# Weight sums on VectorE, lag copies on GpSimd, and three more places for weight spills

## The chip, the cores and the metric

The kernel runs on one core of a Trainium2 chip. The metric is the device time of one execution in microseconds (us). TensorE (PE in the profile) multiplies, with its weight loads shown apart (PEld); VectorE (DVE), ScalarE (ACT) and GpSimd (POOL) do the elementwise work; SyncE (SP) only issues DMA transfers, and GpSimd issues transfers as well. Each engine runs its own instructions strictly in the order in which the program gives them, and waits for other engines by semaphores.

## The reference, cut to what matters

One layer of a streaming encoder on a prompt of 2048 rows and 8 samples of 16 rows, with D_MODEL = 1024:

```python
h = rmsnorm(x, ln_g)
proj = h @ w_in                                   # 1024 -> 5120 columns
u_a, z_a, u_b, z_b, g_a, g_b = split(proj)        # 512, 512, 1024, 1024, 1024, 1024
y_a = s5_mixer(u_a)                               # complex diagonal state space, 32 groups
y_a = gelu(y_a); y_a = y_a * sigmoid(y_a @ w_glu + b_glu)
p_a = (y_a * silu(z_a)) @ w_pa
xc = causal_conv(u_b)                             # width 4
y_b = rglru(xc)                                   # block-diagonal gates, then a scan over time
p_b = (y_b * silu(z_b)) @ w_pb
out = x + (sigmoid(g_a) * p_a + sigmoid(g_b) * p_b) @ w_out
```

Outputs are the normed rows and the new states. All products keep about float32 accuracy: every operand is split into a float16 high part and a float16 low part, and each product is three float16 matmuls (high by high, high by low, low by high; lines 161 to 163).

## The kernel before

The work has stages that follow each other on TensorE: the norm and the S5 inputs; the first gate columns (both up to about 219 us of the profile); sixteen pairs (to about 985 us); the product with w_pb, beside which the S5 recurrence runs (to about 1205 us); and the tail with the GLU, w_pa, w_out and the last norm.

**A pair** (`run_pair`) multiplies the normed input by two blocks of 128 columns of w_in. It does so by Strassen-Winograd's scheme with seven products instead of eight (`quad`, once for each half of the prompt), and between the two halves once for the samples. A pair thus has 15 positions: products 1 to 7, the sample at 8, products 9 to 15. Even pairs ("b") make the input and the gate of branch B, odd pairs ("g") make the merge gates and the S5 gate. Two pairs together number their positions 1 to 30, called `place`: 1 to 15 in a b pair, 16 to 30 in a g pair. Each product goes to one of five PSUM banks; after it, ScalarE or VectorE evicts the bank (tiles `ub`, `gs`, `zb`, `sz`), and a later product takes the bank again.

**The weights of the next pair** are made beside it by the generator `w_forms`. It takes the two raw blocks (`wraw`, float32, 512 columns for each quarter A11, A12, A21, A22) and forms the sums that the scheme wants: S1 = A21 + A22, S2 = S1 - A11, S4 = A12 - S2, S3 = A11 - A21. The first three live in the tile `wt`, the last in A21's place in `wraw`. ScalarE makes the high part of each form (`high`, an ACT copy `wf<-wt` or `wf<-wraw`), VectorE the low part (`low`). The four sums are made by `gtt`, on GpSimd (line 56), 64 in the 16 pairs. The generator advances by one step per position, at 8 to 15 and then at the start of the next pair.

**The planner.** At every position `run_pair` calls `tick(2.8 - c)`: c is the cost that the step of `w_forms` gives with its `yield`, plus a fixed cost of evictions; what is left is the budget from which `pump` starts steps of other jobs. Jobs in `tasks` come first: `b_work`, the convolution taps, gates and scan of branch B (one job per b pair and half, and one for the samples). Jobs in `low` take what remains: `w_spill`, which splits 44 blocks of the later weights into high and low and stores them to DRAM (`wr` loaded, `wq` made on ScalarE and VectorE, stored by a GpSimd DMA), and two `s5_prep` generators, which make the matrices of the 16 S5 group pairs. `Later(k)` lets a job rest k positions, `Step(c)` charges c and lets it rest one. The budget decides only in which order instructions are put on the engines' queues.

A job of `s5_prep` makes two outer products on GpSimd (`wb`, `wc`: each four products into the tile and into `t`, and a sum), transposes and small matmuls on TensorE, splits on ScalarE and VectorE, and stores to `sD` and `kpD`. Its `lags` copies the lag kernel `dd`, loaded back from `kpD`, into another order of columns (`d2`, shown as `d<-dd`): two ScalarE copies of 128x512 float16 per group pair, 32 in all, each reading in steps of 16 elements, and then one GpSimd DMA to `sD`.

Two ranges hold jobs back: `w_spill` does not go on while `place` is in `NO_SPILL` (13 to 21), `s5_prep` not while it is in `NO_PREP` (11 to 21). After pair 15 the loop over w_pb starts with `y_load`, which loads branch B's output `Y` from DRAM through SP's queue.

Of the kernel before, what the change touches and what calls it, by code (L numbers as in the profile page):

```python
# [13 lines left out]
MUL, ADD, SUB, MAX, MIN = ALU.mult, ALU.add, ALU.subtract, ALU.max, ALU.min  # L14
# [33 lines left out]
def build(tc, I, O):  # L48
    nc = tc.nc
    V, S, G, PE, SP = nc.vector, nc.scalar, nc.gpsimd, nc.tensor, nc.sync  # L50

    def tt(out, a, b, op):
        V.tensor_tensor(out=out, in0=a, in1=b, op=op)

    def gtt(out, a, b, op):
        G.tensor_tensor(out=out, in0=a, in1=b, op=op)  # L56
# [7 lines left out]
    def stt(out, a, s, b, op0, op1):  # L64
        V.scalar_tensor_tensor(out=out, in0=a, scalar=s, in1=b, op0=op0, op1=op1)  # L65
# [7 lines left out]
    def act(out, a, f, **kw):  # L73
        S.activation(out=out, in_=a, func=f, **kw)  # L74

    def scopy(out, a, scale=1.0):
        act(out, a, AF.Copy, scale=scale)

    with ExitStack() as es:
# [5 lines left out]
        def ps(tag, shape=(P, 512)):  # L85
            tag = "a" if tag == "b" else tag
            bufs = {"mm": 5, "a": 3}[tag]
            return psp.tile(list(shape), F32, tag=tag, name="ps_" + tag, bufs=bufs)
# [113 lines left out]
        def proj(W, n, tag="mm"):  # L202
            p = ps(tag)[:, :TILES[n][1]]
            gemm(p, W, lambda k: hT(n, k), KB)
            return p
# [9 lines left out]
        with ExitStack() as p1x:  # L215
# [328 lines left out]
            for n in range(4):  # L544
# [8 lines left out]
                for m in range(4):  # L553
                    p = proj(lambda k: wua[m][:, k], n)
# [33 lines left out]
                    if n == 3:  # L588
                        SP.dma_start(out=uD[1024 * m:1024 * m + 1024].rearrange("(p t) x -> p (t x)", t=8),
                                     in_=uE[m].rearrange("p t l j c -> p (t l j c)"))  # L590
# [18 lines left out]
        def gt(shape, dt=F32, name="g"):  # L609
            return gp.tile(list(shape), dt, tag="g", name=name, bufs=slots)  # L610
# [156 lines left out]
        def w_half():  # L767
            return page_a("w", (4, 4, 2, P), "wf")
# [4 lines left out]
        def w_forms(raw, W):  # L773

            r1, r2 = raw
            A11, A12, A21, A22 = r1[:, 0:4], r1[:, 4:8], r2[:, 0:4], r2[:, 4:8]
            t = wp.tile([P, 4, P], F32, tag="wt", name="wt", bufs=1)
            for h in range(2):
                W[h] = None

            def high(nm, src):
                h, i = FORMS[nm]
                if W[h] is None:
                    W[h] = w_half()
                scopy(W[h][:, i, :, 0], src, WS)

            def low(nm, src):
                h, i = FORMS[nm]
                stt(W[h][:, i, :, 1], src, WS, W[h][:, i, :, 0], MUL, SUB)

            high("A11", A11)
            gtt(t, A21, A22, ADD)
            yield 0.1
            low("A11", A11)
            high("S1", t)
            yield 0.7
            low("S1", t)
            gtt(t, t, A11, SUB)
            high("A12", A12)
            yield 0.7  # L800
            low("A12", A12)
            high("S2", t)
            yield 0.7
            low("S2", t)
            gtt(t, A12, t, SUB)
            yield 0.7
            high("A21", A21)
            high("S4", t)
            yield 0.2
            low("A21", A21)  # L810
            gtt(A21, A11, A21, SUB)
            low("S4", t)
            yield 1.4
            high("S3", A21)
            high("A22", A22)
            yield 0.2
            low("S3", A21)
            low("A22", A22)
            yield 1.3
# [308 lines left out]
        def busy(no):  # L1128

            return branch_b and place in no  # L1130

        NO_SPILL = range(13, 22)
        NO_PREP = range(11, 22)

        def w_spill():
# [15 lines left out]
            def load(i):  # L1151
                src, _, nk = blocks[i]
                if branch_b:
                    r = gt([P, nk, 512 // nk], name="wr")
                else:
                    r = raw_tile()[:, 0:4].rearrange("p a b -> p (a b)").rearrange("p (k c) -> p k c", k=nk)
                SP.dma_start(out=r, in_=src)
                return r

            nxt = None  # L1160
            for i, (_, dst, nk) in enumerate(blocks):
                done["spill"] = i
                while busy(NO_SPILL):
                    yield Later(1)
# [4 lines left out]
                nxt = None if branch_b or i + 1 == len(blocks) else load(i + 1)  # L1169
                while busy(NO_SPILL):  # L1170
                    yield Later(1)
# [24 lines left out]
        def s5_prep(second):  # L1196

            def lags(q, dd):
                d2 = gt([P, 2, 4, P], F16, name="d2")
                for j in range(2):  # L1200
                    scopy(d2[:, j].rearrange("p a (h t) -> p a h t", t=8),
                          dd.rearrange("p g l (j t h) -> p j (g l) h t", j=2, t=8)[:, j])
                G.dma_start(out=sD[q, :, 2], in_=d2.rearrange("p j a x -> p (j a x)"))
                prepared.add(q)

            dd = None
            while second and not prepared:
                yield Later(1)
            while todo:
# [35 lines left out]
                p = ps("a", (P, 4, P))  # L1245
# [6 lines left out]
                if dd:  # L1252
                    lags(*dd)
# [35 lines left out]
                dd = q, gt([P, 2, 2, 256], F16, name="dd")  # L1289
                for g in range(2):  # L1290
                    for l in range(2):
                        kk = kpD[q, g, :, l, 128:384]
                        SP.dma_start(out=dd[1][:, g, l],
                                     in_=bass.AP(kk.tensor, kk.offset, [list(kk.ap[0]), [-16, 8], list(kk.ap[1])]))
                yield Step(0.4)
            yield Later(4)
            lags(*dd)


# [31 lines left out]
        raw = load_pair(0)  # L1331
        Ws = {0: {}}
        wg = w_forms(raw, Ws[0])
        for n in range(NT):
            if n == 1:
# [17 lines left out]
        def run_pair(i, hook):  # L1353
# [5 lines left out]
            def slot():  # L1359
                nonlocal pos, wg, place  # L1360
                pos += 1
                place = (0 if kind == "b" else 15) + pos
                cost = 0.0
                if pos <= 4:
                    cost += next(wg, 0)
                elif i + 1 < len(order):
                    if pos == 5:
                        Ws[i + 1] = {}
                        wg = w_forms(load_pair(i + 1), Ws[i + 1])
                    elif pos >= 8:  # L1370
                        cost += next(wg)
                hook(pos, cost + EVICT[kind][pos % 8])
# [287 lines left out]
        for n in range(NT):  # L1660
            w = TILES[n][1]
            for m in range(8):
# [4 lines left out]
                p = ps("mm")[:, :w]  # L1667
# [5 lines left out]
                g = gbl.pop(0)  # L1673
# [190 lines left out]
```

## Time and profile before

| what | value |
|---|---|
| median of 3 runs (lowest to highest) | 1551.13 us (1546.92 to 1555.46) |
| the profiled execution: its time, its span | 1549.53 us, 1547.7 us |
| mean granted TensorE clock | 0.979 |
| TensorE matmul busy | 1446.3 us (93%) |
| VectorE busy | 1034.2 us (67%) |
| ScalarE busy | 815.5 us (53%) |
| GpSimd busy | 505.3 us (33%) |

The span runs from the first to the last instruction; the execution's own time has 1.83 us more around it. Busy shares are means over stages with different limits, so the stages are read one by one.

### The profile page before, as it was taken

The page shows a single profiled execution, that of the slowest core. Times are in us where ns is not written, and L with a number is a line of the kernel's source. Part 1 is how long each engine was busy: PE and PEld are TensorE (multiplying, and loading weights), DVE is VectorE, ACT ScalarE, POOL GpSimd, SP SyncE. Part 2 cuts the span into 40 slices and gives each one's busy share as a digit, 9 for nine tenths or more (in the row PEclk, how much of TensorE's full clock was granted, in tenths as well). Part 3 has the DMA queues.
Part 4 walks back from the last instruction along what each step waited for, and adds up shares of the span by engine and source line. Part 5 has one row for each costly group of instructions (what it writes and reads, how often), then busy time and mean ns, then how long its engine had stood idle before and what let it go on. Part 6 is the DMA issues. An engine that isn't in the chain of part 4 may idle for free.

```text
span 1547.7 us, 22800 instructions
## 1 busy us (share of the span) xinstructions
PE 1446.3 (93%) x8168; PEld 724.0 (47%) x8168; DVE 1034.2 (67%) x1913; ACT 815.5 (53%) x1526; POOL 505.3 (33%) x781
## 2 busy tenths in 40 slices
PE   7999999999899999998898899799999899999998
PEld 4544445444444444444443444355555544454444
DVE  5546768867588686887768777444445696665543
ACT  7642446757577575874856758423222562542322
POOL 0790133444536444274363642223332200000000
PEclk9999999999999999999999999899999899999999
DMA  8325223332423424241333241998766772163521
GB/s 207 106 92 208 89 77 93 102 122 86 140 82 109 130 86 140 76 158 61 104 127 92 87 134 69 324 360 292 251 214 221 265 255 72 70 219 107 177 82 55
DMA packets 168490, 222.21 MB, mean 144 GB/s; under 512 B 39258, under 2 KB 117738, under 8 KB 166328
## 3 DMA queue, kind: packets, MB, share of 16 engines
q1 hardware_dynamic: 144440, 150.96, 30.8%
q0 software_dynamic: 23936, 69.79, 12.0%
q8 instruction: 64, 1.05, 0.3%
q14 instruction: 50, 0.41, 0.1%
HBM read 133.85 MB, written 86.84 MB: 143 GB/s over the span
## 4 chain that ended last, share of the span: by engine, by line
PE 48%; issue 15%; DVE 11%; POOL 10%; ACT 7%; DMA 7%; SPq 2%; POOLq 0%; DVEq 0%; ACTq 0%
PE ps_mm L161 11%; PE ps_mm L163 11%; PE ps_mm L162 11%; PE ps_mm L1773 4%; PE ps_mm L1771 4%; PE ps_mm L1772 4%; DVE xc L65 2%; POOL wt L56 2%; POOL t L56 2%; POOL wc L56 1%; POOL wb L56 1%; DVE wf L65 1%; ACT L74 1%; POOL wraw L56 1%; ACT d L74 1%
## 5 line engine op out<-in xcount | busy, mean ns | idle before, releaser
L161 PE MATMUL ps_mm<-T,wf 128*128 128x512 f16 x512 | 198.8, 388 | 34.8 <-ACT gs L74 23.0
L163 PE MATMUL ps_mm<-T,wf 128*128 128x512 f16 x512 | 198.7, 388 | 1.3 <-DVE wf L65 1.3
L162 PE MATMUL ps_mm<-T,wf 128*128 128x512 f16 x512 | 198.6, 388 | 0.0
L162 PEld LDWEIGHTS <-wf 128*128 128x128 f16 x1232 | 121.7, 99 | 151.3 <-issue 46.2
L161 PEld LDWEIGHTS <-wf 128*128 128x128 f16 x1232 | 121.8, 99 | 121.6 <-issue 12.0
L163 PEld LDWEIGHTS <-wf 128*128 128x128 f16 x1232 | 121.7, 99 | 119.9 <-issue 7.0
L161 PE MATMUL ps_mm<-h,wf 128*128 128x512 f16 x448 | 171.2, 382 | 2.0 <-ACT wf L74 2.0
L163 PE MATMUL ps_mm<-h,wf 128*128 128x512 f16 x448 | 170.8, 381 | 0.7 <-DVE wf L65 0.7
L162 PE MATMUL ps_mm<-h,wf 128*128 128x512 f16 x448 | 170.8, 381 | 0.0
L161 PE MATMUL ps_mm<-Y,wpb 128*128 128x512 f16 x256 | 98.0, 383 | 11.0 <-DMA Y<-ybD 11.0
L65 DVE SCALAR_TENSOR_TENSOR gb<-gb,ps_mm 128x512 f32<-128x512 f32 (+1 forms) x40 | 24.3, 607 | 115.3 <-PE ps_mm L163 115.3
L1773 PE MATMUL ps_mm<-wo,M 128*128 128x512 f16 (+2 forms) x264 | 98.0, 373 | 3.4 <-DVE M L65 3.4
L1771 PE MATMUL ps_mm<-wo,M 128*128 128x512 f16 (+2 forms) x264 | 98.0, 373 | 0.0
L1772 PE MATMUL ps_mm<-wo,M 128*128 128x512 f16 (+2 forms) x264 | 98.0, 373 | 0.0
L162 PE MATMUL ps_mm<-Y,wpb 128*128 128x512 f16 x256 | 98.0, 383 | 0.0
L163 PE MATMUL ps_mm<-Y,wpb 128*128 128x512 f16 x256 | 97.8, 382 | 0.0
L74 ACT ACT_TABLE_LOAD x64 | 82.1, 1283 | 3.7 <-PE ps_mm L163 1.8
L65 DVE SCALAR_TENSOR_TENSOR xc<-ub,PC,xc 128x512 f32<-128x512 f32 x96 | 79.9, 832 | 3.2 <-ACT xc L74 1.0
L65 DVE SCALAR_TENSOR_TENSOR wf<-wraw,wf 128x512 f16<-128x512 f32 (+1 forms) x82 | 64.8, 806 | 6.2 <-ACT wf L74 6.1
L65 DVE SCALAR_TENSOR_TENSOR xo<-ps_mm,xo 128x512 f32<-128x512 f32 (+2 forms) x35 | 23.6, 674 | 65.4 <-PE ps_mm L1773 65.4
L1065 POOL DMA_DIRECT2D gbD<-gs x40 | 21.8, 546 | 134.4 <-ACT gs L74 134.3
L74 ACT ACTIVATE yo<-ps_a 128x256 f32<-128x256 f32 x64 | 14.7, 281 | 86.1 <-PE ps_a L1479 86.0
(323 smaller groups left out, 3529.2 us busy)
## 6 DMA issues: line engine op xcount, KB each, us to landing
wraw<-w_in SPq DMA_DIRECT2D x38, 512.0 KB, 4.4
sp<-sD SPq DMA_DIRECT2D x16, 768.0 KB, 4.9
xt<-x_prompt SPq DMA_DIRECT2D x16, 512.0 KB, 4.2
gbD<-gs POOLq DMA_DIRECT2D x32, 256.0 KB, 2.3
ybD<-y POOLq DMA_DIRECT2D x32, 256.0 KB, 2.8
gaD<-gs POOLq DMA_DIRECT2D x32, 256.0 KB, 2.5
Y<-ybD SPq DMA_DIRECT2D x8, 1024.0 KB, 9.9
gb<-gbD SPq DMA_DIRECT2D x32, 256.0 KB, 6.9
```

Of the source, the lines that this page charges most:

```text
L56: G.tensor_tensor(out=out, in0=a, in1=b, op=op)
L65: V.scalar_tensor_tensor(out=out, in0=a, scalar=s, in1=b, op0=op0, op1=op1)
L74: S.activation(out=out, in_=a, func=f, **kw)
L161: PE.matmul(p, lhsT=a[:, 0], rhs=b[:, 0], start=first, stop=False, skip_group_check=more)
L162: PE.matmul(p, lhsT=a[:, 0], rhs=b[:, 1], start=False, stop=False, skip_group_check=more)
L163: PE.matmul(p, lhsT=a[:, 1], rhs=b[:, 0], start=False, stop=last, skip_group_check=more)
L1065: G.dma_start(out=dst[m, :, t0:t0 + w], in_=t)
L1771: PE.matmul(p, lhsT=lh[0], rhs=w_[:, 0, c], start=(k == 0), stop=False)
L1772: PE.matmul(p, lhsT=lh[0], rhs=w_[:, 1, c], start=False, stop=False)
L1773: PE.matmul(p, lhsT=lh[1], rhs=w_[:, 0, c], start=False, stop=(k == KB - 1))
```

## The change

The four sums of `w_forms` go from GpSimd (`gtt`) to VectorE (`tt`), and the cost that each of those steps reports to the planner rises by 0.6. The range in which spills rest shrinks from places 13 to 21 to places 15 to 20, so that they may go on at 13, 14 and 21 too. The two copies in `lags` go from ScalarE to GpSimd.

```diff
             high("A11", A11)
-            gtt(t, A21, A22, ADD)
-            yield 0.1
+            tt(t, A21, A22, ADD)
+            yield 0.7
             low("A11", A11)
             high("S1", t)
             yield 0.7
             low("S1", t)
-            gtt(t, t, A11, SUB)
+            tt(t, t, A11, SUB)
             high("A12", A12)
-            yield 0.7
+            yield 1.3
             low("A12", A12)
             high("S2", t)
             yield 0.7
             low("S2", t)
-            gtt(t, A12, t, SUB)
-            yield 0.7
+            tt(t, A12, t, SUB)
+            yield 1.3
             high("A21", A21)
             high("S4", t)
             yield 0.2
             low("A21", A21)
-            gtt(A21, A11, A21, SUB)
+            tt(A21, A11, A21, SUB)
             low("S4", t)
-            yield 1.4
+            yield 2.0
...
-        NO_SPILL = range(13, 22)
+        NO_SPILL = range(15, 21)
...
                 for j in range(2):
-                    scopy(d2[:, j].rearrange("p a (h t) -> p a h t", t=8),
-                          dd.rearrange("p g l (j t h) -> p j (g l) h t", j=2, t=8)[:, j])
+                    G.tensor_copy(out=d2[:, j].rearrange("p a (h t) -> p a h t", t=8),
+                                  in_=dd.rearrange("p g l (j t h) -> p j (g l) h t", j=2, t=8)[:, j])
```

## Rows read from the trace of the kernel before

**Rows 1.** Windows: us, busy (instructions) of each engine, clock, DMA share, GB/s.
```profile
219.00:985.00 766.00, 711.91 (x3949) 348.16 (x3948) 575.55 (x869) 513.94 (x900) 352.03 (x453) 0.98 0.34 110
985.00:1205.00 220.00, 210.02 (x1388) 115.96 (x1387) 102.39 (x324) 60.25 (x185) 67.94 (x112) 0.98 0.78 271
```
**Rows 2.** TensorE's waits: us in total, times, longest.
```profile
PE ps_mm L161 <- ACT gs L74: 23.0, 11, 5.8
PE ps_mm L161 <- DMA Y<-ybD: 11.0, 2, 9.3
PE ps_mm L161 <- ACT ub L74: 10.3, 7, 3.5
PE ps_a L162 <- DVE xs L53: 7.3, 4, 4.3
```
**Rows 3.** All engines' waits, two of them.
```profile
ACT wf L74 <- POOL wt L56: 48.7, 27, 4.9
...
POOL sD L1203 <- ACT d L74: 27.0, 12, 4.2
```
**Rows 4.** Timeline of ScalarE in pair 13: start, us, [idle before, releaser].
```profile
872.74 0.63 ACT L74 ACTIVATE wf<-wt 128x512 f16<-128x512 f32 x1 [4.68 <-POOL wt L56]
...
878.21 2.13 ACT L74 ACTIVATE d<-dd 128x512 f16<-128x512 f16 x2
880.24 0.59 ACT L74 ACTIVATE gs<-ps_mm 128x512 f32<-128x512 f32 x1
```
**Rows 5.** Timeline of GpSimd in the same stretch.
```profile
866.30 1.75 POOL L56 TENSOR_TENSOR wc<-par 128x256 f32<-128x256 f32 x2
...
871.44 1.26 POOL L56 TENSOR_TENSOR wt<-wraw 128x512 f32<-128x512 f32 x1
```
**Rows 6.** Timeline of TensorE: first and last of nine waits.
```profile
391.70 0.58 PE L161 MATMUL ps_mm<-T,wf 128*128 128x512 f16 x1 [5.83 <-ACT gs L74]
...
929.22 0.38 PE L161 MATMUL ps_mm<-T,wf 128*128 128x512 f16 x1 [3.49 <-ACT ub L74]
```
**Rows 7.** Windows right behind two of those waits, columns as in rows 1.
```profile
880.90:884.40 3.50, 3.50 (x9) 1.29 (x9) 2.25 (x4) 3.47 (x6) 3.48 (x6) 0.50 0.40 151
391.70:396.70 5.00, 5.00 (x12) 1.72 (x12) 2.02 (x4) 4.38 (x8) 4.91 (x7) 0.50 0.26 105
```
**Rows 8.** Groups by line and form: busy us, mean ns | idle before.
```profile
L56 POOL TENSOR_TENSOR wt<-wt,wraw 128x512 f32<-128x512 f32 x16 | 25.7, 1609 | 26.3 <-DVE wf L65 26.2
...
L56 POOL TENSOR_TENSOR wt<-wraw 128x512 f32<-128x512 f32 x16 | 21.1, 1318 | 14.2 <-DMA wraw<-w_in 14.1
```
**Rows 9.** The same view, ScalarE and VectorE.
```profile
L74 ACT ACTIVATE d<-dd 128x512 f16<-128x512 f16 x32 | 34.4, 1127 | 0.8 <-DMA dd<-kpD 0.8
L53 DVE TENSOR_TENSOR gs<-ps_mm,gs 128x512 f32<-128x512 f32 x48 | 32.8, 684 | 16.7 <-PE ps_mm L163 16.4
...
L53 DVE TENSOR_TENSOR ga<-ga,mb 128x512 f32<-128x512 f32 x32 | 22.1, 692 | 1.7 <-DMA mb<-mbD 0.6
```
**Rows 10.** Tiles sz and wq: ns shortest/median/longest, first and last start.
```profile
L65 DVE SCALAR_TENSOR_TENSOR sz<-sz,zb x16: 675/1218/2172, 237.2 to 939.6; 128x512 f32<-128x512 f32 x16
...
L74 ACT ACTIVATE wq<-wr x38: 612/620/637, 222.1 to 986.1; 128x512 f16<-128x512 f32 x38
L65 DVE SCALAR_TENSOR_TENSOR wq<-wr,wq x38: 676/683/3319, 222.9 to 988.7; 128x512 f16<-128x512 f32 x38
```
**Rows 11.** Groups of GpSimd with no second input.
```profile
L386 POOL MEMSET zt<- 128x1024 f16 x1 | 1.0, 953 | 0.0
...
L434 POOL COPY pw<-stk 128x64 f32<-128x64 f32 x1 | 0.3, 299 | 0.0
...
L484 POOL COPY m16c<-SQ 128x16 f32<-128x16 f32 x1 | 0.2, 200 | 0.0
```
**Rows 12.** Timeline of SP's queue at the end of pair 15.
```profile
983.86 2.46 SPq L1293 DMA_DIRECT2D dd<-kpD  x4
986.37 1.14 SPq L1545 DMA_DIRECT2D Y<-ybD  x2
```

## Prediction

> **What bounds the kernel now.** I read the windows by stage first. TensorE is the bound almost everywhere, so what counts is where it stands still. Beside the product with w_pb it is busy 210 of 220 us, in the sixteen pairs 712 of 766 [rows 1]: 54 us of idle time lie in the pairs, and all that the change touches lies there too, save the last six spills. The list of TensorE's waits comes next: most of that idle time is a product that waits for ScalarE to evict its bank (23.0 us for `gs`, 10.3 for `ub`), the rest in part VectorE's `xs` (7.3) [rows 2]. So the question is what makes ScalarE late. In the list of all waits it stands 48.7 us, 27 times, for GpSimd's sum `wt` [rows 3]. The timeline of pair 13 shows how that reaches TensorE. GpSimd runs the second outer product `wc` from 866.30, and the sum that was put on its queue behind it starts at 871.44 [rows 5]. ScalarE waits 4.68 us for it with every eviction queued behind; later the two lag copies take 2.13 us directly ahead of the eviction of `gs` [rows 4], and TensorE stands 5.14 us until 880.88.
>
> I went through TensorE's timeline for the pairs in this way. Nine waits have, in the 9 us ahead of them, a ScalarE wait for a sum or an outer product of GpSimd; the first is 5.83 us and the last 3.49 [rows 6], and the nine sum to 28.2 us. Six of them are followed by a stretch at a granted clock of 0.50, which is 1.2 GHz, the lower of the two levels; the two shown last 3.5 and 5.0 us [rows 7]. A stretch at half clock loses half its length, so six of these lengths lose 10.5 to 15 us; some are shorter, and I take 11.5. Behind these waits stand some 40 us.
>
> **The sums on VectorE.** 64 sums leave GpSimd, in four groups whose means run from 1.32 to 1.61 us [rows 8]: 64 x 1.47, some 94 us. On VectorE the same form, `ga<-ga,mb` with two float32 inputs in SBUF, takes 0.69 us [rows 9]: 64 x 0.69 = 44 us more on an engine that is busy 575 of 766 us in this stage [rows 1].
>
> Part of this comes back. `sz<-sz,zb` with both inputs in SBUF takes 0.675 us at its shortest, 1.218 in the median and 2.172 at the longest, and `wq` 0.683 against 3.319 [rows 10]; `gs<-ps_mm,gs`, one input in PSUM, has a mean of 0.684 [rows 9]. The long ones of the timeline lie over GpSimd's tensor_tensor. So each sum on GpSimd now holds up VectorE's two-input work. VectorE runs 75% of the time; if it stood still for all of that share of 94 us, moving the sums would give back 70 us, if for none of it nothing. I take 40, since the longest rows show a hold for a whole GpSimd instruction but many of VectorE's have an input in PSUM. Net VectorE gains 4 us of work, between 44 more and 26 less.
>
> On the path: the sum follows a `low` on the same queue, so it needs no hop between engines, and the outer products no longer stand in front of it. The nine waits lose their cause. Not all is won: GpSimd's second sum stood 26.2 us of its idle time waiting for VectorE's `low` [rows 8], so VectorE's own lag stays in the chain, and ScalarE's head-of-line wait becomes a wait for VectorE. I leave a quarter of the 28.2 us in place: 7 us. Queued behind each sum are taps, splits and evictions. Where VectorE is late already, at the gates in b pairs (`xs`, four waits, longest 4.3 [rows 2]), one sum in front costs 0.69 in each of 8 b pairs: 5.5 us. If instead two of the four sums lay on the path in all 16 pairs it would be 22 us; if none, nothing.
>
> **The planner's costs.** The nine steps of `w_forms` report 6.0 before and 8.4 after. Two pairs have 30 x 2.8 = 84 of budget; less two `w_forms` and the fixed evictions (10.7) that leaves 61.3, now 56.5. `b_work` needs 37.1 of it by its own costs, spills 44 / 8 x 1.0 and two preps 2 x 3.6, together 12.7. It still fits, so the jobs move by single positions and none falls out; the added VectorE work displaces other work instead of piling up on it. Price 0. If the last prep slips, its loads of `dd` stand in front of `Y` on SP's queue, as they do today by 2.5 us [rows 12], and TensorE already waits 11.0 us for `Y` [rows 2]: each position of slip would add 2.6 us, and a slip past `y_load` would put `Y` first and give back up to 11. I take 0, with both ends kept.
>
> **The lag copies on GpSimd.** ScalarE loses 32 copies of 1.127 us, 34.4 us [rows 9]. What one costs on GpSimd no row shows. From below, the memset writes 1024 elements in 0.953 us, so 0.48 us for 512; the two copies of 64 and 16 elements give 0.099 / 48 = 2.06 ns for an element [rows 11] and so 0.200 + 496 x 0.00206 = 1.22 us; from above, the slowest group of two-input sums, 1.61 us [rows 8]. I take the copies' value: 32 x 1.22 = 39 us, between 15 and 52. GpSimd then has 94 - 39 = 55 us less to do. It used to wait 27.0 us for ScalarE's copies before the DMA to `sD` [rows 3]; that wait goes, and the copies take about its place. What stands behind them are the next `wc` and the stores. The DMA itself is hidden: `sD` is read only after 985 us. The relief of ScalarE is already in the nine waits (pair 13 has both causes), so I count it once, at nothing extra; uncovered, it would be worth up to 2.13 us where the copies stand ahead of an eviction.
>
> The Trainium skill speaks against this part ("SBUF — State Buffer", § Who interferes with whom): a VectorE instruction with two SBUF inputs contends with a GpSimd instruction that reads SBUF, and the second to issue blocks until the first is done. The long `sz` rows agree for tensor_tensor [rows 10]; for a GpSimd copy no run here shows it. By it the copies too would hold VectorE's two-input work; without it they would cost VectorE nothing.
>
> **The spills.** 38 of 44 blocks are split in the pairs, each 0.62 us of ScalarE and 0.68 of VectorE [rows 10], one load on SP's queue and one store on GpSimd's. With 24 of 30 places open instead of 21, the other six should move into the pairs. Beside the w_pb product they cost nothing today, as TensorE is busy there; in the pairs they cost 6 x 0.68 = 4 us if all lay on the path. VectorE's 190 us of idle time cover them: price 0.
>
> **The sum.** 1549.5 - 28.2 - 11.5 + 7 + 5.5 = 1522.3 us for the profiled execution. The median of the runs is 1.6 us above that execution: 1524.
>
> **The rivals.** *Half eaten.* VectorE's lag takes over ScalarE's wait, and reordering makes new waits at other places. For: the `low` in front of each sum, and `xs` late already. Against: in pair 13 and at others of the nine places VectorE stood idle itself, waiting for ScalarE in its turn. Half to all of 40 us is lost: 1531 to 1551, 1541 at the middle.
>
> *More than forecast.* With GpSimd lighter by 55 us the waits for `wb` and `wc` go too, taps shorten, and `Y` slips in front: 54 + 13 us is the ceiling, of which half of what my forecast leaves would give about 1503.
>
> *VectorE becomes the bound (the other side).* Two of four sums in each pair lie on the path, held by the outer products (2.17 us as the longest `sz` instead of 0.69): 16 x 2 x 0.69 to 2.17 = 22 to 69 us; and the lag copies hold VectorE as the sums do now, for up to 75% of their 39 us, 29 us. Against the 40 us won this ends between 1533 and 1610; with 65 us of new waits it is 1576. It turns slower once the new waits exceed 40 us, 2.5 per pair. For it: an engine 75% busy that gets more to do, and taps that GpSimd already stretches. Against it: the 40 us handed back, and the budget that makes room.
>
> **How the numbers follow.** Forecast (1510 to 1536) 0.45; half eaten 0.22; more than forecast 0.12; VectorE bound 0.21. The range reaches from 1500, about where the larger gain lies, over all of the second case to 1557, leaving out some 0.04 below and 0.16 above. A difference under 0.5%, 8 us, is about what this kernel's measurement can't tell from no change. Faster by more than that, below 1543: all of the forecast, all of the larger gain and half of the second case, 0.68. Same: the other half and 0.05 of the third, 0.16. Slower, above 1559: 0.16.
>
> **What would show it.** Right: `ACT wf <- POOL wt` is gone from the waits and what replaces it, `ACT wf <- DVE wt`, is under 25 us; TensorE's wait for `gs` falls below 10 us; fewer stretches at clock 0.50 in the pairs; `sz<-sz,zb` nearer 0.7 us; lag copies near 1.2 us; VectorE's busy time in the pairs within 25 us of 575; all spills before 985. Wrong: TensorE's waits for `xs` or for VectorE's evictions grow beyond 20 us, or VectorE is over 620 us busy; the lag copies take 2 us or more; `Y` starts later behind `dd`.

## The result, and the profile after

The changed kernel takes 1524.52 us (median of 4 runs, 1523.57 to 1527.46); the kernel before takes 1551.02 (4 runs). The ratio is 0.9832 with a 95% interval of 0.9801 to 0.9862. The profiled execution of after took 1527.46 us with a span of 1525.7, against 1547.7.

The 22.0 us between the two spans come from the pairs. Read from TensorE's timeline (first and last products of each stage), the pairs take 733.8 us instead of 765.9, 32.1 less. The stages ahead, in which only the first two of the 64 sums lie, ended 5.5 us later in this execution, at 223.2 us; that varies between executions, as e7_no_lags, the same kernel up to there, ended them at 218.5; the gap between the last pair's product and the first with `Y` grew from 9.7 to 13.3 us; the w_pb stage and the tail differ by -0.1 and +1.2.

The windows of the pairs and of the w_pb stage, which answer to [rows 1]:

```profile
223.00:957.00 734.00, 705.04 (x3943) 346.24 (x3939) 576.65 (x923) 482.34 (x864) 279.73 (x405) 0.98 0.34 111
957.00:1195.00 238.00, 221.40 (x1559) 126.40 (x1559) 113.66 (x341) 65.29 (x196) 91.25 (x143) 0.97 0.81 281
```

VectorE has 54 instructions more in the pairs and is busy 576.65 us, 1.1 more than before. GpSimd gives up 72 us, ScalarE 32.

TensorE's waits (us in total, times, longest), which answer to [rows 2]:

```profile
PE ps_mm L161 <- DMA Y<-ybD: 10.1, 2, 8.9
PE ps_a L162 <- DVE xs L53: 7.7, 3, 3.7
PE ps_mm L161 <- DVE gs L53: 7.3, 3, 4.3
...
PE ps_mm L161 <- ACT gs L74: 5.3, 1, 5.3
...
PE ps_mm L161 <- ACT ub L74: 0.2, 1, 0.2
```

The waits for ScalarE's `gs` and `ub`, 33.3 us before, are 5.5. `xs` stands where it stood; TensorE's wait for VectorE's part of `gs` has grown to 7.3 (1.4 in the pairs before). In the list of all waits ScalarE no longer waits for GpSimd's `wt` (48.7 us in [rows 3]), but for VectorE's:

```profile
ACT wf L74 <- DVE wt L53: 17.1, 16, 3.8
```

Tiles of after (ns shortest/median/longest, first and last start), for [rows 10] and the operation that no row of before had:

```profile
L65 DVE SCALAR_TENSOR_TENSOR sz<-sz,zb x16: 676/683/1074, 241.3 to 909.7; 128x512 f32<-128x512 f32 x16
...
L1201 POOL COPY d<-dd x32: 1096/1116/1581, 314.0 to 1013.4; 128x512 f16<-128x512 f16 x32
...
L74 ACT ACTIVATE wq<-wr x37: 612/617/634, 229.1 to 965.7; 128x512 f16<-128x512 f32 x37
L74 ACT ACTIVATE wq<-wraw x7: 612/629/632, 997.1 to 1124.4; 128x512 f16<-128x512 f32 x7
```

`sz` is back at its shortest. A lag copy takes 1.12 us in the median. But the spills did not move in: 37 blocks are split from `wr` in the pairs (38 before), and the last of the seven behind them begins at 1124.4.

So the number came out as forecast. Whether it came by the forecast steps, only the parts can tell.

### The profile page after: what moved, and what is told of

The parts are those of the page before. It is cut to its first block, busy times and chain, and to the rows that moved or that the text cites. A ratio compares the mean times of both kernels' runs of the same rounds, so it can differ in the third digit from the quotient of the medians.

```text
span 1525.7 us, 22740 instructions
## 1 busy us (share of the span) xinstructions
PE 1445.7 (95%) x8168; PEld 726.4 (48%) x8168; DVE 1043.5 (68%) x1977; ACT 785.1 (51%) x1494; POOL 446.1 (29%) x749
## 3 DMA queue, kind: packets, MB, share of 16 engines
q1 hardware_dynamic: 144440, 150.96, 31.1%
q0 software_dynamic: 23936, 69.79, 12.3%
## 4 chain that ended last, share of the span: by engine, by line
PE 69%; DVE 11%; DMA 6%; ACT 5%; issue 5%; POOL 3%; SPq 1%; DVEq 0%; POOLq 0%; ACTq 0%
PE ps_mm L161 17%; PE ps_mm L163 17%; PE ps_mm L162 17%; PE ps_mm L1773 4%; PE ps_mm L1772 4%; PE ps_mm L1771 4%; DVE wf L65 1%; ACT L74 1%; DMA xt<-x_prompt 1%; ACT yh L74 1%; DVE xc L65 1%; DMA kpD<-kf 1%; DMA Y<-ybD 1%; DMA wraw<-w_in 1%; SPq L1293 1%
## 5 line engine op out<-in xcount | busy, mean ns | idle before, releaser
L162 PEld LDWEIGHTS <-wf 128*128 128x128 f16 x1232 | 121.4, 99 | 126.1 <-issue 18.9
L161 PE MATMUL ps_mm<-Y,wpb 128*128 128x512 f16 x256 | 97.7, 382 | 10.1 <-DMA Y<-ybD 10.1
L74 ACT ACTIVATE gs<-ps_mm 128x512 f32<-128x512 f32 (+1 forms) x92 | 48.3, 534 | 34.9 <-PE ps_mm L163 31.1
```

Source lines behind the costliest of these rows:

```text
L161: PE.matmul(p, lhsT=a[:, 0], rhs=b[:, 0], start=first, stop=False, skip_group_check=more)
L162: PE.matmul(p, lhsT=a[:, 0], rhs=b[:, 1], start=False, stop=False, skip_group_check=more)
```

## The experiments

The change is cut into four: **S**, the sums on VectorE (`gtt` to `tt`); **C**, the costs in the `yield` lines of `w_forms`; **L**, the lag copies on GpSimd; **P**, the three more places for spills. In the table, "effect" is (ratio - 1) x 1552 us, the median of before in these comparisons. "Pairs" and "w_pb" are lengths of stages from TensorE's timeline. "Idle" sums TensorE's waits of over 0.3 us in the pairs. "Half clock" sums what its successive 128x512 products there lose by starting about 0.43 us apart instead of 0.216. The last four are worked out from the trace of one execution each.

| kernel | parts | median | ratio (95%) | effect | pairs | w_pb | idle | half clock |
|---|---|---|---|---|---|---|---|---|
| before | none | 1552 | 1 | 0 | 765.9 | 224.5 | 53.0 | 14.9 |
| e1_sums | S | 1542.97 | 0.9939 (0.9917, 0.9960) | -9.5 | 755.7 | 226.2 | 41.4 | 14.3 |
| e3_lags | L | 1561.44 | 1.0067 (1.0047, 1.0088) | +10.4 | 774.3 | 224.1 | 56.0 | 19.6 |
| e2_costs | C | 1553.74 | 1.0006 (0.9990, 1.0023) | +0.9 | 750.4 | 236.8 | 46.8 | 5.9 |
| e4_spill | P | 1551.70 | 0.9993 (0.9977, 1.0010) | -1.1 | 765.3 | 224.6 | 51.1 | 16.0 |
| e9_engines_only | S L | 1550.86 | 0.9981 (0.9964, 0.9997) | -2.9 | 763.2 | 227.0 | 45.0 | 19.2 |
| e5_sums_costs | S C | 1551.37 | 0.9985 (0.9975, 0.9995) | -2.3 | 750.8 | 237.1 | 37.3 | 15.2 |
| e8_order_only | C P | 1533.34 | 0.9876 (0.9854, 0.9897) | -19.2 | 741.4 | 224.2 | 36.6 | 9.1 |
| e6_no_spill_part | S C L | 1536.13 | 0.9897 (0.9881, 0.9914) | -16.0 | 737.0 | 238.0 | 29.8 | 12.0 |
| e7_no_lags | S C P | 1520.08 | 0.9788 (0.9765, 0.9811) | -32.9 | 729.5 | 224.6 | 27.9 | 6.7 |
| after | S C L P | 1524.52 | 0.9832 (0.9801, 0.9862) | -26.1 | 733.8 | 224.4 | 28.4 | 10.8 |
| e10_dummy | S + load | 1553.65 | 1.0011 (0.9994, 1.0027) | +1.7 | 765.0 | 225.5 | 48.7 | 17.0 |
| e12_dummy_new_order | S C P + load | 1527.81 | 0.9833 (0.9809, 0.9858) | -25.9 | 739.2 | 223.3 | 31.1 | 11.6 |
| e11_y_early | S C P, `Y` early | 1517.53 | 0.9762 (0.9743, 0.9782) | -36.9 | 729.9 | 230.6 | 28.3 | 7.0 |

**e1_sums: the sums alone.** The four `gtt` become `tt`, the costs stay:

```diff
-            gtt(t, A21, A22, ADD)
+            tt(t, A21, A22, ADD)
             yield 0.1
...
```

> The kernel before with the four weight sums on VectorE and nothing else: the planner's costs stay as they were, so every engine's order is that of before, with 64 sums moved from GpSimd's queue into VectorE's. Theory (ScalarE's wait for sums that stand behind outer products on GpSimd is the cause): ScalarE's wait for wt falls from 48.7 us to under 25, TensorE's for gs from 23.0 to under 10, the time by 15 to 35 us (ratio 0.977 to 0.990). Rival A (the gain comes from the planner putting the work in another order): under 8 us, ratio above 0.995. Rival B (VectorE becomes the bound unless the planner makes room): slower than before, ratio above 1.005.

9.5 us are won, a third of what the prediction gave this part, and a size between the ranges of the recorded theory and of rival A. TensorE's waits and the window of the pairs:

```profile
PE ps_a L162 <- DVE xs L53: 18.2, 5, 5.3
...
PE ps_mm L161 <- ACT ub L74: 9.6, 7, 3.1
...
PE ps_mm L161 <- ACT gs L74: 5.6, 11, 2.2
```
```profile
218.00:974.00 756.00, 712.81 (x3960) 348.89 (x3958) 574.03 (x930) 512.38 (x899) 264.80 (x393) 0.98 0.34 111
```

The wait for `gs` goes as forecast, 23.0 to 5.6. VectorE has 61 instructions more in the pairs and is busy 574.03 us where it was 575.55, so the 40 us that were to come back came back. But `xs` grows from 7.3 to 18.2. The longest of its waits, 5.32 us in pair 12, on the timelines of VectorE and of GpSimd:

```profile
813.62 1.12 DVE L65 SCALAR_TENSOR_TENSOR wf<-wt,wf 128x512 f16<-128x512 f32 x1
814.78 1.01 DVE L53 TENSOR_TENSOR wt<-wt,wraw 128x512 f32<-128x512 f32 x1
815.71 1.75 DVE L53 TENSOR_TENSOR xs<-xc,xs 128x512 f16<-128x512 f32 x1
```
```profile
813.11 2.12 POOL L56 TENSOR_TENSOR t<-par 128x256 f32<-128x256 f32 x2
815.31 1.60 POOL L56 TENSOR_TENSOR wb<-wb,t 128x512 f32<-128x512 f32 x1
```

The sum stands directly ahead of `xs`, and GpSimd's outer product, which is not moved, lies over all three and stretches `xs` to 1.75 us. And the clock falls behind such a wait as it fell behind those for ScalarE: the window right after the 4.29 us for `xs` in pair 10 is at 0.50, the lower level (1.2 GHz).

```profile
711.10:715.50 4.40, 4.40 (x11) 1.49 (x11) 4.29 (x10) 2.73 (x6) 0.58 (x1) 0.50 0.08 27
```

So the half-clock loss stays: 14.3 us, 14.9 before.

The orders of all engines are those of before, so each of the prediction's nine waits can be looked up at its own product. Together they are 28.2 us before and 8.3 here.

**e10_dummy: is it that GpSimd is free of the sums?** As e1_sums, and GpSimd is given its load back without the dependence: four additions of a small tile of zeros beside each sum, which nothing reads.

```diff
+            for _ in range(4):
+                gtt(dmy, dmy, dmy, ADD)
             tt(t, A21, A22, ADD)
```

> As the kernel with the sums alone on VectorE, but beside each sum GpSimd gets four idle additions of 80 float16 zeros on a tile of its own, together about 1.4 us, at the place in its queue where the sum was; nobody waits for them. GpSimd's load and its hold on VectorE's second input stay about as before, ScalarE's wait for GpSimd is gone. Theory (the queue wait is the cause): at most a third of the gain of the sums alone is lost. Rival C (the gain is VectorE set free from GpSimd's sums): at least two thirds of it are lost.

The whole gain goes (+1.7, interval from -0.9 to +4.2), though nothing reads what is added. The load is larger than the one taken away: GpSimd is busy 132 us longer in the pairs than in e1_sums, where the sums had taken 87. VectorE is busy 10.5 us longer. TensorE's waits:

```profile
PE ps_a L162 <- DVE xs L53: 14.3, 5, 4.7
PE ps_a L172 <- POOL wb L56: 11.8, 3, 6.8
```

By the total this is rival C's case, but the waits say otherwise. At the nine products TensorE waits 11.6 us here (28.2 before, 8.3 in e1_sums), so most of what ScalarE's wait for the sums had cost stays won. The loss lies elsewhere. Most of it is `wb`, 11.8 us for 2.2 in e1_sums: outer products that come late on GpSimd's own queue. Before, with the real sums on that queue, TensorE waited only 2.8 us for `wb`, so the additions, half as much load again, are no fair stand-in for the sums. If the loss of 11.2 us is scaled from 132 us to 87, 7.4 of the 9.5 us that the sums gave would be GpSimd's lighter load; that is an estimate that takes the loss as proportional to the load, which no run shows.

**e3_lags: the lag copies alone.**

```diff
-                    scopy(d2[:, j].rearrange("p a (h t) -> p a h t", t=8),
-                          dd.rearrange("p g l (j t h) -> p j (g l) h t", j=2, t=8)[:, j])
+                    G.tensor_copy(out=d2[:, j].rearrange("p a (h t) -> p a h t", t=8),
+                                  in_=dd.rearrange("p g l (j t h) -> p j (g l) h t", j=2, t=8)[:, j])
```

> The kernel before with the lag copies on GpSimd and nothing else; orders unchanged. Theory: ScalarE is 36 us less busy, GpSimd's sums come later by about 2.4 us where copies stand ahead of them, so the nine waits stay: within 6 us of before (ratio 0.996 to 1.004). Rival D (the copies ahead of evictions were the larger cause of late banks): 10 us faster or more. Rival E (the copies hold VectorE): 8 us slower or more.

10.4 us slower. The window of the pairs, then two waits of TensorE and one of ScalarE:

```profile
218.00:993.00 775.00, 718.92 (x3964) 350.03 (x3962) 608.64 (x867) 484.09 (x870) 385.49 (x485) 0.97 0.33 109
```
```profile
PE ps_mm L161 <- ACT gs L74: 20.0, 11, 4.4
...
PE ps_a L161 <- DVE wbT L65: 8.0, 3, 3.9
```
```profile
ACT wf L74 <- POOL wt L56: 66.9, 32, 4.9
```

Rival E is met. VectorE has two instructions fewer than before and is busy 33 us longer. The copies' hold can be seen at single instructions, here of VectorE and of GpSimd:

```profile
936.69 2.89 DVE L53 TENSOR_TENSOR xs<-xc,xs 128x512 f16<-128x512 f32 x1
```
```profile
936.88 2.14 POOL L1201 COPY d<-dd 128x512 f16<-128x512 f16 x2
```

`xs`, both inputs in SBUF, takes 0.68 us in the median with GpSimd idle, and 2.89 over two copies. Fifteen such instructions lie over copies and no other GpSimd operation; together they last 18.9 us longer than the medians of their kind. `gs<-ps_mm,gs`, one input in PSUM, keeps its 0.69 us over a copy. ScalarE's wait for sums grows from 48.7 to 66.9, since the copies stand ahead of them, and TensorE waits 8.0 us for VectorE's `wbT` (1.9 before).

**e9_engines_only: S and L, orders unchanged.** The diffs of e1_sums and e3_lags together.

> Sums on VectorE and lag copies on GpSimd, with the planner's costs and the spill places of before: orders unchanged, so this is the change without its reordering. Theory: as the sums alone or up to 8 us faster, since ScalarE's copies stood ahead of evictions in four of the nine waits; ratio 0.975 to 0.988. Rival A (reordering makes the gain): ratio above 0.993.

-2.9 us: the copies take 6.5 of the 9.5 that the sums give. What the two moves between engines do by themselves is a tenth of the result, as rival A has it; the rest comes only with the planner's edits.

**e2_costs, e4_spill, e8_order_only: the planner's half.** All instructions stay on their engines. e2_costs has the first hunk below, e4_spill the second, e8_order_only both.

```diff
-            yield 0.1
+            yield 0.7
...
-            yield 1.4
+            yield 2.0
...
-        NO_SPILL = range(13, 22)
+        NO_SPILL = range(15, 21)
```

> The kernel before with only the planner's costs of the changed kernel. Costs and spill places together gave 19 us with no move between engines, while with sums and costs but the old places the last spill came at 1207 us and the w_pb stage took 237 us instead of 224. Theory 3 (the costs spread the two preps and the branch work more evenly, which helps the pairs, but push spills out of them, which the new places bring back): the pairs are 10 us or more shorter than 766, the w_pb stage 8 to 14 us longer, the total within 10 us of before. Rival H (the places alone make the gain): the pairs take over 760 us.

> The kernel before with only the new range of spill places. Theory 3: spills fit in the pairs already, so the places bring little by themselves: within 8 us of before, ratio 0.995 to 1.005. Rival H (the places alone make the gain): 12 us faster or more, ratio under 0.992.

> The planner's costs and the spill places of the changed kernel, but sums on GpSimd and lag copies on ScalarE as before: the reordering without the moves between engines. Theory 2: ScalarE still waits for sums, TensorE's waits for gs stay above 15 us, within 8 us of before (ratio 0.995 to 1.005). Rival A (reordering makes the gain): 15 us faster or more, ratio under 0.990.

Each alone gives nothing; together they give 19.2 us. The costs shorten the pairs by 15.5 us (6.2 of idle time and 9.0 of half clock) and lose 12.3 of it in the w_pb stage, as theory 3 has it. The tile `wq` and TensorE's waits of e2_costs show where:

```profile
L74 ACT ACTIVATE wq<-wr x33: 612/614/642, 227.1 to 972.9; 128x512 f16<-128x512 f32 x33
L74 ACT ACTIVATE wq<-wraw x11: 612/630/631, 996.2 to 1208.7; 128x512 f16<-128x512 f32 x11
```
```profile
PE ps_mm L161 <- ACT yh L74: 14.4, 1, 14.4
PE ps_a L172 <- POOL wb L56: 14.1, 6, 2.7
PE ps_mm L161 <- ACT gs L74: 10.7, 6, 3.8
```

The dearer steps leave less budget for `low`, and 11 blocks instead of 6 are left behind the pairs. There they go one at a time, (1208.7 - 996.2) / 10 = 21 us apart. The generator of the tail goes on only when all are done (`while len(tasks) > 1 or done["spill"] < 44`, line 1627), so `yh` is 14.4 us late. With the three places open, 37 blocks fit into the pairs, the last of the others begins at 1131.2, and the w_pb stage is back at 224.2.

The pairs' own gain is one of order: one block fewer is split there than before, and the pairs are 24.5 us shorter. ScalarE waits for GpSimd's sums as long as before, and still TensorE's waits for `gs` are a third, against theory 2, which had them above 15 us (all waits of e8_order_only, then TensorE's timeline at the longest and ScalarE's just ahead of it):

```profile
ACT wf L74 <- POOL wt L56: 50.8, 27, 6.3
...
PE ps_mm L161 <- ACT gs L74: 7.9, 2, 5.4
PE ps_mm L161 <- ACT ub L74: 7.1, 5, 3.8
```
```profile
485.84 0.59 PE L161 MATMUL ps_mm<-T,wf 128*128 128x512 f16 x1 [5.45 <-ACT gs L74]
```
```profile
482.68 0.58 ACT L74 ACTIVATE wbT<-ps_a 128x512 f16<-128x512 f32 x1
483.16 2.15 ACT L74 ACTIVATE d<-dd 128x512 f16<-128x512 f16 x2
485.21 0.58 ACT L74 ACTIVATE gs<-ps_mm 128x512 f32<-128x512 f32 x1
```

I placed the starts of the outer products among the positions. Before, pairs 3, 11 and 13 have one at place 24 or 25 and another at 28; those are the pairs with the waits of 5.83, 4.13 and 5.14 us ahead of the product at place 28. With the new order pair 5 alone has that pattern, and the 5.45 us above are pair 5 ahead of place 28; the next there is 2.41 us. The second outer product starts only when the wait is over (in pair 13 at 881.75, TensorE's product at 880.88), so it is the mark of a second prep, not what the bank waits for. What that prep puts on ScalarE is what stands there: in all four pairs its split `wbT` and two lag copies run directly ahead of the late eviction, and the wait for a sum comes some 7 us earlier. The two causes can be taken apart at the three products, as e1_sums and e3_lags keep the orders: without the wait for GpSimd's sums 0.90, 0.00 and 2.20 us are left, without the copies on ScalarE 3.82, 2.10 and 3.43. That the new order wins by keeping the second prep out of such g pairs is argued from the match; no kernel moves a prep alone.

**e5_sums_costs, e6_no_spill_part, e7_no_lags: pairs of parts and one left out.** e5 is S and C, e6 is after without P, e7 is after without L, each with the hunks shown above.

> The kernel before with the sums on VectorE and the planner's costs of the changed kernel; lag copies and spill places as before. The sums alone gave 9 us: TensorE's waits for gs fell from 23.0 to 5.6 us, but its waits for xs grew from 7.3 to 18.2. Theory 2 (the move pays when the planner also makes room on VectorE for it): the xs waits fall back under 10 us and the gain is 18 to 30 us, ratio 0.981 to 0.988. Rival F (the spill places carry the rest): about the sums alone, ratio 0.991 to 0.997.

> The changed kernel with the old range of spill places. Theory 2: the places are worth little, within 6 us of the changed kernel, ratio 0.979 to 0.989. Rival F (the places carry much of the gain): 10 us or more slower than the changed kernel, ratio above 0.990.

> The changed kernel with the lag copies back on ScalarE. They cost 9 us when moved alone and 8 us when moved beside the sums. Theory 2, with the copies' price the same here: 5 to 10 us faster than the changed kernel, ratio 0.976 to 0.981. Rival G (with ScalarE's queue free of GpSimd's sums, the relief of ScalarE shows): slower than the changed kernel by 4 us or more, ratio above 0.986.

e5_sums_costs fails both of its ranges: 2.3 us are won, and `xs` is still 15.8. Without P the w_pb stage is 237 to 238 us in both e5 and e6 (14.6 and 14.8 us of waiting for `yh`): P is worth 10.1 us in the whole change (e6 to after), near rival F's size: 13.6 in the w_pb stage and 3.2 in the pairs, some of it given back in the gap before `Y` and in the start. With L left out P is worth three times as much, 30.6 us (e5 to e7), and 21.3 of them are in the pairs: 9.4 of idle time and 8.5 of half clock. In e5 and e6 each of the six b pairs from pair 4 on has a wait for `xs` of 2.3 to 3.9 us at place 12; with P two such waits of over 2 us are left in e7 and in after. Why the spill places do this is not traced. Without L the kernel is 4.4 us faster by the medians, 6.8 by the ratios, whose intervals touch at 0.9801 and 0.9811; theory 2 had 5 to 10. Its pairs are 4.3 us shorter, and VectorE is busy 558.72 us there for 576.65. At one product after waits 5.34 us where e7 waits 2.45, here on the timelines of GpSimd, ScalarE, VectorE and TensorE:

```profile
543.93 2.95 POOL L1201 COPY d<-dd 128x512 f16<-128x512 f16 x2 [4.03 <-PE ps_mm L163]
...
548.25 2.13 POOL L1201 COPY d<-dd 128x512 f16<-128x512 f16 x2
...
546.92 0.81 ACT L74 ACTIVATE xc<-ub,PC 128x512 f32<-128x512 f32 x1 [3.05 <-POOL d L1201]
...
547.76 4.75 DVE L65 SCALAR_TENSOR_TENSOR xc<-ub,PC,xc 128x512 f32<-128x512 f32 x3 [1.84 <-ACT xc L74]
...
552.12 0.59 PE L161 MATMUL ps_mm<-T,wf 128*128 128x512 f16 x1 [5.34 <-ACT gs L74]
```

By the profile ScalarE's first tap waits for a pair of copies, with the eviction of `gs` queued behind it, and TensorE stands 5.34 us. The three taps on VectorE take 4.75 us over the second pair of copies.

**e12_dummy_new_order: e10's load in the new order.** e7_no_lags with the added lines of e10_dummy.

> Sums on VectorE, costs and spill places of the changed kernel, lag copies on ScalarE, and the idle additions on GpSimd beside each sum again. Without the additions this took 1520.1 us, with the sums on GpSimd 1533.3. Theory 4 (GpSimd's load itself is what the sums cost, by its hold on VectorE and by the lateness of its other work; ScalarE's wait is the smaller part): at least half of the 13 us is lost, 1526 us or more. Theory 1 again (ScalarE's wait for the sum): under a third is lost, 1524 or less.

In the new order S is worth 13.7 us (e8 to e7), and the idle additions take 7.0 of them back (0.9788 to 0.9833; the intervals touch at 0.981). They load GpSimd with 123 us, where the sums had taken 98 (347.16 us busy in e8, 249.11 in e7), and VectorE's busy time grows by 1.3 us only. Theory 4 is met, by little. In proportion to the load, an estimate as above, GpSimd's lighter load would be 5.6 of the 13.7. Where it acts is not shown: TensorE's waits for `wb` and `xs` are those of e7 (6.4 and 9.5 us, 6.2 and 9.6 there), and what grows is idle time in many places, 3.2 us, and half clock, 4.9. What makes up the other 8 us of S in this order is not taken apart either.

**e11_y_early: the first load of `Y` ahead of the last `dd`.** e7_no_lags with

```diff
-            if pos == 13:
+            if pos == 11:
                 y_load(0)
```

> Sums on VectorE, costs and spill places of the changed kernel, lag copies on ScalarE, and the first load of Y two positions earlier (11 instead of 13), ahead of the last prep's loads of dd on SP's queue. Theory (Y waits there behind dd, which waits for a store): TensorE's wait for Y falls from 8.5 us to under 3, the time by 5 to 11 us to 1509 to 1515, ratio 0.972 to 0.976. Rival (the 6 MB of loads bound it): Y lands no earlier, ratio as without it, 0.979.

SP's queue of e11_y_early has `Y` first now:

```profile
942.44 1.24 SPq L1545 DMA_DIRECT2D Y<-ybD  x2
...
952.66 2.56 SPq L1293 DMA_DIRECT2D dd<-kpD  x4
```

The gap to the first product with `Y` falls from 14.5 to 7.7 us, but the w_pb stage grows by 6.0, and 2.6 us are won by the medians, with intervals that overlap: the forecast of 1509 to 1515 is missed, though TensorE's wait for `Y` falls under 3 us as it said. What was hidden behind the wait shows behind it, an outer product first:

```profile
972.43 0.42 PE L1274 MATMUL ps_a<-wc,par 128*32 128x128 f32 x1 [3.35 <-POOL wc L56]
```

By its median it is the fastest kernel of the study, and ahead of after with intervals that don't meet (up to 0.9782, from 0.9801).

## Why the prediction was right, and where it was not

The forecast of 1524 us is met, within the narrow range too, but not by its steps: that it hits the median is luck. Its two prices were -27.2 for the sums and 0 for the rest. Along one path through the runs (none, C P, S C P, all) the parts are -19.2 for the planner, -13.7 for the sums and +6.8 for the lag copies, -26.1 in all. Three errors cancel. The split depends on the path: by none, S, S C, S C P, all it is -9.5, +7.2, -30.6 and +6.8. No part has a price of its own that holds beside every other.

**The nine waits: right.** With the sums alone they fall from 28.2 to 8.3 us, and 7 were to be left (all waits for `gs` and `ub` fall from 33.3 to 15.2). The cause that was named is borne out: in e10_dummy, with GpSimd's queue loaded otherwise, the nine are 11.6. But the gain is not S's alone. At the same nine products e8_order_only, with the sums still on GpSimd, waits 2.6 us, and e2_costs 4.9: the new order takes these waits away as well, and they can be won only once.

**The `xs` waits: half.** +5.5 was forecast for 0.69 us of a sum in each b pair; +10.9 came (e1_sums), since the outer products hold VectorE as well, and the sum and `xs` are stretched. In after `xs` is 7.7 us; the order that C and P make together keeps it down, as the kernels with S that lack one or both have 18.2, 17.0, 15.8 and 20.7 (e1, e9, e5, e6).

**The half clock: wrong in size.** -11.5 was counted as won with the nine waits; -0.6 came with the sums alone and -4.1 in after. The low clock followed the waits for `xs` as it had those for `gs` (0.50 behind both), so the waits that replaced the old ones brought it along. The sum of idle time does not tell how much: e2_costs has 46.8 us of it and 5.9 of half clock, after 28.4 and 10.8. This is the most mis-sized of the four terms that had a price.

**VectorE's balance: right.** 44 us added and 40 given back were to make +4; e1_sums measures -1.5, with 61 instructions more.

**The planner's costs and the spills at price 0: the step that failed.** "It still fits, so the jobs move by single positions and none falls out", and from that "Price 0". Blocks do fall out (33 instead of 38 in the pairs, e2_costs), which costs 12.3 us behind the pairs, and the new order is worth 15.5 us in them; with P, e8_order_only wins 19.2 us where the sum had nothing. The sum of the budget, 56.5 us for 49.8 of work, said that all fits; it could not say which step meets which. That "the other six should move into the pairs" failed too: seven stay out. P keeps C from pushing out more, and it changes the order in the pairs (9.0 us shorter beside C, e2 to e8).

**The lag copies at price 0: wrong.** Their duration was right (1.12 us in the median against 1.22). They cost 10.4 us alone, 6.5 beside S and 4.4 to 6.8 in the whole. VectorE is busy 33 us longer in e3_lags, 23 in e9_engines_only (beside e1_sums) and 18 in after (beside e7_no_lags); the bound was 29. That is what spoke against them: by the Trainium skill's "SBUF — State Buffer", § Who interferes with whom, a VectorE instruction with two SBUF inputs contends with a GpSimd instruction that reads SBUF. The traces agree for a copy (2.89 us for 0.68 in e3_lags). The hold was left to the rival in which VectorE becomes the bound; it belonged into the sum.

**The rivals.** The total is that of the forecast case. "Half eaten" is what the sums alone do (1543), and "more than forecast" is not reached. VectorE as the bound is what e9_engines_only comes near: S and L by themselves end at 0.9981, 2.9 us and so inside the 8 us that the prediction would not tell from no change. **`Y`** stayed behind `dd`, with its gap 3.6 us longer; e11_y_early shows that of the up to 11 us named for it 2.6 were there to be had.

**The signs.** Of those named as right, all came but one: ScalarE's wait for `wt` of GpSimd is gone, the wait for `wt` of VectorE is 17.1 (under 25), `gs` for ScalarE 5.3 (under 10), `sz` 0.683, the copies 1.12, VectorE 1.1 us from 575.55, and half clock is less, if by less than counted; but the spills are not all done before 985. None of those named as wrong came, except that `Y` is a little later. The signs could not tell where the gain was from: e8_order_only has `gs` under 10 as well, with every instruction on its old engine.

**Open.** L beside S and C without P helps by 13.7 us (e5 to e6), where it costs in the three other settings. Idle time in the pairs falls by 7.5 us of that, half clock by 3.2. The wait for `ub`, 6.9 us in e5 and none in e6, is the largest that goes; that ScalarE's copies stood ahead of those evictions is likely, but not traced. That C and P together shorten the pairs by 8.4 us more than the two alone do, and that P shortens them by 21.3 beside S and C, is not traced either. P with S or with L, and C with L, were not run.

## What to carry to other kernels

A total that comes out as forecast does not show that its terms did; here each had to be run, alone and beside the others. Where a planner interleaves jobs by reported costs, a changed cost is an edit of its own, and often the larger one: run it alone and with the engines as before, and look at what its budget pushes past the next barrier. Take the time that a slow clock costs off a forecast only for waits that nothing replaces. When work moves to GpSimd, price it twice: on its own queue, and as a hold on VectorE's instructions with two inputs in SBUF that run beside it.

## What the runs showed of the hardware

A GpSimd copy of 128x512 float16, reading in steps of 16 elements, takes 1.10 us at its shortest, about what ScalarE takes for it (1.127 [rows 9]). It holds VectorE though it has one input: in e3_lags 32 copies, 35.7 us busy, go with 33 us more of VectorE's busy time for the same work; VectorE's instructions with an input in PSUM keep their 0.69 us. The short additions of e10_dummy, 80 elements of float16, take 0.53 us each in the mean (256 of them, 134.6 us), where the 512-element sums took 1.3 to 1.6 [rows 8]; for 132 and 123 us of load they hold VectorE little (10.5 us in e10_dummy, 1.3 in e12_dummy_new_order).
